# The first feed-forward of a hybrid encoder step begun with half of its token blocks

## Chip, cores and metric
One core of a Trainium2 chip runs the whole program in one launch. The metric is the device time of an execution in microseconds (us), from the median of three runs for the kernel before. TensorE, VectorE, ScalarE (ACT), GpSimd (POOL) and SyncE (SP, which issues the DMAs) run beside each other and wait for each other on semaphores.

## The reference, cut to what matters
A one-layer encoder step on 1088 tokens (1024 of a prompt, conditioned on one vector, and 64 of a sample, on another), 1024 features, in float32:

```
mod = silu(c) @ w_ada + b_ada            -> shift, scale, gate for 3 sub-layers
h   = rms_norm(x, gain) * (1 + scale) + shift
x  += 1/2 * gate * (silu(h @ Wg) * (h @ Wu)) @ Wd          (first half-step, width 2816)
x  += gate * (stick-breaking attention and retention, 8 + 4 heads) @ w_out
x  += 1/2 * gate * the same kind of feed-forward            (second half-step)
```

The change is in the opening of the two feed-forwards: norm, modulation, and the first tiles of `h @ [Wg Wu]`.

## The kernel before, in words
Activations lie feature-major: `A[k]` holds 128 features by 1088 tokens, for k of 0 to 7. The tokens are cut into four blocks of 272 (`BL`), numbered 0 to 3. Every float32 operand of a product is split into a high part (a cast by ACT, L81 and L228) and a low part (the difference, on POOL at L86 for weights and on VectorE at L229 for activations), and each product is three matmuls (`mm3`, L198 to L202).

The up-projection (class `Up`, L449) multiplies by Strassen-Winograd: k is halved (k and k+4), the tokens are paired (blocks 0 and 1 with blocks 2 and 3: half s=0 of a product is the columns of blocks 0 and 2, half s=1 those of blocks 1 and 3), and the outputs are paired as gate and up. A tile f (22 of them) has seven products in the order p1, p6, p5, p7, p2, p4, p3 (`ORDER`, L34), each for two halves s, each of 4 k by 3 matmuls of 272 columns. Its operands are seven combinations of activation blocks (b11, t1, t2, b21, t3, t4, b22; `x_parts`, L403), built once, and seven of weights per tile (`prep`, L477: four loads of 256 KB, four sums on VectorE at L469, seven splits). `read` (L511) takes a product out of PSUM with adds on VectorE (L521), copies and Silu on ACT (L533, L537, L546) and multiplies gate and up (L527).

Four raw and seven split weights fit, so one tile's weights are live at a time and the next tile's take the places as its products end.

In the opening of the first feed-forward (L628 to L726) SP loads x in three chunks of columns (`CHUNKS`, 24 loads), 16 loads of 512 KB of the modulation weights, of which four fit at a time (tag au), and the weights of tile 0. ACT squares x (L265), POOL and VectorE add the squares (L268), TensorE sums them over the partitions (`fold`), POOL takes the power (`factors`, L218), and TensorE spreads the row factors over the partitions (`rows`, L224), chunk after chunk. VectorE scales all of A by them (`scaled`, L673). TensorE makes the shift and scale vectors kt by kt (`ada_sums`, L681; `ada_turn`, L692; VectorE takes them at L685, L695, L697). `x_build_whole` (L432) builds the operands of one k for all four blocks at once, 544 columns wide: ACT applies scale and shift (L419), VectorE makes the differences (L424), and each of the seven is split. Behind each k, TensorE runs that k of p1, p6 and p5 of tile 0 for both halves. Then the remaining products of tile 0 and the tiles 1 to 21 follow with both halves of each product in turn; tiles 1 to 18 share VectorE with 64 long products for the later modulation vectors (`Ada`, L754).

The opening of the second feed-forward (L1308 to L1431) is cut by blocks already: operands of blocks 0 and 2 first (`build_first`), and at L1405 to L1431 tile 0 and tile 1 on half 0, tile 1 and tile 0 on half 1, with the weights of tile 0 split again for the last.

The order of the instructions on each engine is made by the scheduler of the program's framework, by the written order as priority and by what it takes to be ready. Inside `manual_schedule(engines={PE})` TensorE keeps the written order; the other engines don't. `high_priority(offset=2000)` moves the priority of what is in it 2000 steps ahead.

Of the kernel before, what the change touches and what calls it, by code (L numbers as in the profile page):

```python
# [8 lines left out]
F32 = mybir.dt.float32  # L9
# [106 lines left out]
def tile_hybrid_step(ctx: ExitStack, tc: tile.TileContext, I, O):  # L116
# [133 lines left out]
    class Norm:  # L250
# [92 lines left out]
    def ada_bias(s):  # L343
        bias = tiny.tile([P, KT], F32, tag="bias", name=f"bias{s}", bufs=2)
# [47 lines left out]
    def x_whole(pool):  # L392

        tags = [(hpool, f"{t}{k}") for k in range(KT) for t in "HL"] + [(pool, f"xe{i + 2}") for i in range(4)]
        for k in range(4):
            for i, name in enumerate(("b11", "b21", "t3", "t4", "b22", "t2", "t1")):
                if i < 5:
                    p, tag = tags[5 * k + i]
                else:
                    p, tag = xpool, f"A{k + 4 * (i - 5)}"  # L400
                yield k, name, p, tag

# [29 lines left out]
    def x_build_whole(k, n, pool, places):  # L432

        h = 2 * BL
        b = x_parts([(name, kt, lo, A[kt][:, lo:lo + h], None) for name, kt, lo in
                     (("b11", k, 0), ("b12", k, h), ("b21", k + 4, 0), ("b22", k + 4, h))], pool, n, k, "", True)
        for name in ("b11", "t2", "t1", "t3", "b21", "t4", "b22"):
            p, tag = places[k, name]
            t = p.tile([P, NTOK], F32R, tag=tag, name=f"x{name}{k}", bufs=1)
            split_h(b[name], t[:, :h], t[:, h:], nc.vector)  # L440
            for part in range(2):
                for s in range(2):
                    X[name, part, k, s] = t[:, (2 * part + s) * BL:(2 * part + s + 1) * BL]

    def x_split(b, names, k, s):
        for name in names:
            split_h(b[name], X[name, 0, k, s], X[name, 1, k, s], nc.vector)

# [110 lines left out]

    class Down:  # L560
# [68 lines left out]
    places = {(k, name): (p, tag) for k, name, p, tag in x_whole(xe)}  # L629
    up = Up(1, I["wup1"], hd[:FFT])  # L630
    with tc.tile_pool(name="st", bufs=1, reuse_waits="tile") as pool:
# [6 lines left out]

        def ada_load(kt):
            for s in (1, 0):  # L640
                t = adau[s, kt] = pool.tile([P, D], F32, tag="au", name=f"au{s}_{kt}", bufs=4)
# [16 lines left out]
        for kt in PAIRS[2:]:  # L658
            ada_load(kt)
        nc.sync.dma_start(qkg, I["qkg"])  # L660

        ns = [Norm(0, c, pool, ("pj", "z", "wt")[c]) for c in range(3)]

        def norm_first(c):
            ns[c].fold()
            ns[c].factors()
            ns[c].rows(("pj", "z", "wt")[c])

        def scaled(c, kts):

            c0, w = CHUNKS[c]
            for kt in kts:
                nc.vector.tensor_tensor(A[kt][:, c0:c0 + w], A[kt][:, c0:c0 + w], ns[c].rb[:, :w], op=ALU.mult)  # L673
# [881 lines left out]
```

## Time and profile before

| | us |
|---|---|
| median of 3 runs (lowest, highest) | 2296.6 (2291.3, 2299.8) |
| the profiled execution: its time | 2298.47 |
| its span, first to last instruction | 2296.7 |
| TensorE busy | 2184.1 (95%) |
| VectorE busy | 1503.6 (65%) |
| GpSimd busy | 1051.9 (46%) |
| ScalarE busy | 844.5 (37%) |

The busy time of TensorE is that of matmuls which overlap in the pipeline. The mean granted clock of the span is 0.979 of 2.4 GHz. A line such as "L202 PE MATMUL p<-xt,wh1s" names the line of the kernel, the engine, the operation, and the tiles it writes and reads by their names in the program.

### The profile page before, as it was taken

Reading aid. Unit: us, or ns where it says so; the run is one execution under the profiler, and the core shown is the slowest. Engines: PE = TensorE matmul, PEld = TensorE weight load, DVE = VectorE, ACT = ScalarE, POOL = GpSimd, SP = SyncE. Lnnn points to the kernel's source line nnn. Section 1 sums busy time; section 2 is a strip of 40 time slices with the busy share of each in tenths; the row PEclk is TensorE's granted clock in tenths of the full one; section 3 lists DMA queues with packets and bytes.
Section 4 is the critical chain, followed back from the end, with each engine's and each line's share of the span. In section 5 each row is a group of like instructions: output and inputs, shape, how many; then the busy total and the mean of one; then the engine's idle time right before and its main releaser. Section 6 shows DMA issues by size and latency. Waiting matters only on the chain.

```text
span 2296.7 us, 40613 instructions
## 1 busy us (share of the span) xinstructions
PE 2184.1 (95%) x15356; PEld 2140.8 (93%) x15356; DVE 1503.6 (65%) x2934; ACT 844.5 (37%) x1755; POOL 1051.9 (46%) x989
## 2 busy tenths in 40 slices
PE   5899999999999988888999999998999999999999
PEld 4899999999999988887888998997999999999999
DVE  6767677655787777787775446576555555556666
ACT  5533322332221336665664334365323232322211
POOL 3444444453454556444344445554544444534442
PEclk9899999999999989999999999999999999999999
DMA  7233333336344311110101112432222222352323
GB/s 249 93 126 126 116 127 113 131 108 218 119 129 132 120 52 61 35 41 21 44 22 62 37 41 77 153 99 92 95 85 94 84 90 81 108 178 84 101 82 103
DMA packets 119492, 225.63 MB, mean 98 GB/s; under 512 B 14848, under 2 KB 55808, under 8 KB 119296
## 3 DMA queue, kind: packets, MB, share of 16 engines
q1 hardware_dynamic: 119296, 223.03, 30.0%
q8 instruction: 121, 1.98, 0.4%
q14 instruction: 75, 0.61, 0.1%
HBM read 180.12 MB, written 42.86 MB: 97 GB/s over the span
## 4 chain that ended last, share of the span: by engine, by line
PE 80%; DVE 8%; POOL 4%; issue 4%; ACT 3%; DMA 1%; SPq 0%; POOLq 0%; DVEq 0%; ACTq 0%
PE p L201 13%; PE p L200 13%; PE p L202 13%; PE dn L200 8%; PE dn L201 7%; PE dn L202 7%; PE pj L200 3%; PE pj L202 3%; PE pj L201 3%; DVE f L961 2%; DVE s L964 1%; ACT f L953 1%; PE av L1006 1%; POOL rh L218 1%; PE wt L995 1%
## 5 line engine op out<-in xcount | busy, mean ns | idle before, releaser
L246 DVE SCALAR_TENSOR_TENSOR A<-dn,mod,A 128x384 f32<-128x384 f32 (+1 forms) x704 | 329.8, 497 | 147.7 <-PE dn L202 147.2
L200 PE MATMUL dn<-hs,wh 128*128 128x384 f32 (+1 forms) x1056 | 348.6, 330 | 5.2 <-DVE A L246 5.2
L201 PE MATMUL dn<-hs,wl 128*128 128x384 f32 (+1 forms) x1056 | 348.0, 330 | 0.0
L202 PE MATMUL dn<-hl,wh 128*128 128x384 f32 (+1 forms) x1056 | 347.8, 329 | 0.0
L86 POOL TENSOR_TENSOR wl<-wr,wh 128x512 fp32r<-128x512 f32 x178 | 242.9, 1373 | 143.2 <-ACT wh L81 140.0
L200 PE MATMUL pj<-Hh,wh 128*128 128x384 f32 (+1 forms) x672 | 237.8, 354 | 2.5 <-DVE A L246 2.5
L229 POOL TENSOR_TENSOR hl<-hr,hs 128x384 fp32r<-128x384 f32 x132 | 132.3, 1019 | 235.1 <-ACT hs L228 219.7
L202 PE MATMUL pj<-Lh,wh 128*128 128x384 f32 (+1 forms) x672 | 224.3, 334 | 0.0
L201 PE MATMUL pj<-Hh,wl 128*128 128x384 f32 (+1 forms) x672 | 223.3, 332 | 0.0
L200 PEld LDWEIGHTS dn<-hs,wh 128*128 128x128 f32 x1056 | 199.0, 188 | 5.6 <-DVE A L246 5.5
L201 PEld LDWEIGHTS dn<-hs,wl 128*128 128x128 f32 x1056 | 199.0, 188 | 0.0
L202 PEld LDWEIGHTS dn<-hl,wh 128*128 128x128 f32 x1056 | 199.0, 188 | 0.0
L228 ACT CAST hs<-hr 128x384 fp32r<-128x384 f32 x132 | 65.3, 496 | 326.6 <-PE dn L201 161.6
L521 DVE TENSOR_TENSOR u<-p,p 128x272 f32<-128x272 f32 x176 | 77.4, 440 | 161.2 <-PE p L202 161.2
L81 ACT CAST wh<-wr 128x512 fp32r<-128x512 f32 x178 | 107.7, 619 | 133.3 <-PE dn L202 39.5
L200 PE MATMUL p<-xt,wh1s 128*128 128x272 f32 x528 | 153.8, 291 | 0.9 <-DVE u L521 0.9
L202 PE MATMUL p<-xt,wh1s 128*128 128x272 f32 x528 | 153.6, 291 | 0.6 <-DVE xt L229 0.4
L201 PE MATMUL p<-xt,wl1s 128*128 128x272 f32 x528 | 153.8, 291 | 0.0
L86 POOL TENSOR_TENSOR wl1a<-wr1a,wh1a 128x512 fp32r<-128x512 f32 x66 | 94.1, 1427 | 120.8 <-ACT wh1a L81 120.8
L86 POOL TENSOR_TENSOR wl2a<-wr2a,wh2a 128x512 fp32r<-128x512 f32 x69 | 91.7, 1330 | 108.8 <-ACT wh2a L81 106.9
L200 PEld LDWEIGHTS pj<-Hh,wh 128*128 128x128 f32 x672 | 129.4, 193 | 5.5 <-issue 3.5
L201 PEld LDWEIGHTS pj<-Hh,wl 128*128 128x128 f32 x672 | 129.6, 193 | 0.3
(311 smaller groups left out, 6711.3 us busy)
## 6 DMA issues: line engine op xcount, KB each, us to landing
wa<-in_wada SPq DMA_DIRECT2D x56, 512.0 KB, 3.7
hd<-hh SPq DMA_DIRECT2D x44, 544.0 KB, 2.8
wr2a<-in_wup SPq DMA_DIRECT2D x92, 256.0 KB, 2.7
wr1a<-in_wup SPq DMA_DIRECT2D x88, 256.0 KB, 2.8
wr<-in_wdn SPq DMA_DIRECT2D x88, 256.0 KB, 2.9
hr<-hd SPq DMA_DIRECT2D x88, 192.0 KB, 2.6
wr<-in_win SPq DMA_DIRECT2D x56, 256.0 KB, 2.7
wr<-in_wout SPq DMA_DIRECT2D x34, 256.0 KB, 2.9
```

The costliest lines, as they stand in the source:

```text
L81: self.nc.scalar.copy(h, raw)
L86: self.nc.gpsimd.tensor_tensor(l, raw, h.bitcast(F32), op=ALU.subtract)
L200: nc.tensor.matmul(ps[:, :w], wh, xh, start=first, stop=False, skip_group_check=read_between)
L201: nc.tensor.matmul(ps[:, :w], wl, xh, start=False, stop=False, skip_group_check=read_between)
L202: nc.tensor.matmul(ps[:, :w], wh, xl, start=False, stop=last, skip_group_check=read_between)
L218: nc.gpsimd.tensor_tensor(out, a[:k, :n], neghalf[:k, :n], op=ALU.pow)
L228: nc.scalar.copy(hi, src)
L229: eng.tensor_tensor(lo, src, hi.bitcast(F32), op=ALU.subtract)
L246: nc.vector.scalar_tensor_tensor(A[d][:, s0:s0 + sw] if out is None else out[:, s0 - c0:s0 - c0 + sw], ps[:, s0 - c0:s0 - c0 + sw], mod[:, ...
L521: nc.vector.tensor_tensor(new(name), ps[:, :BL], v[y, s], op=ALU.add)
L953: nc.scalar.activation(t[:rows, end - k0:end - k0 + w], z[:rows, :w], AF.Sigmoid, scale=qsc[self.p][:rows, k, 2 * i + e:2 * i + e + 1])
L961: nc.vector.tensor_tensor_scan(fr[:, ::-1], fr[:, ::-1], fr[:, ::-1], 1.0, op0=ALU.mult, op1=ALU.bypass)
```

## The change
The first feed-forward is opened as the second is. x is loaded by blocks, 0 and 2 first; their norm, scaling, modulation and operands come first (`norm_first(0)`, `build(k, 0)`), and TensorE runs p1, p6 and p5 of tile 0 on half 0 behind each k. Then come norm and operands of blocks 1 and 3 (`norm_first(1)`, `build(k, 1)`), beside `up_first`: the rest of tile 0 and tile 1 on half 0, tile 1 and then tile 0 on half 1, with tile 0's weights prepared a second time. The operands of a pair of blocks are built 544 columns wide in fewer buffers (U twice, T once). The second feed-forward calls `up_first` too; there its first three products are now written ahead of their reads, and the reads of the two half-0 passes get a raised priority. The later modulation products go to tiles 2 to 19 instead of 1 to 18.

```diff
-            sq = self.pool.tile([P, 384 if self.n < 2 else w], F32, tag="acc" if new else "sq",
-                                name=f"sq{self.n}_{self.c}_{d}", bufs=4 if new else 3)
+            tag, bufs = ("v", 12) if self.n == 0 else ("acc", 4) if new else ("sq", 3)
+            sq = self.pool.tile([P, 384 if self.n == 1 else w], F32, tag=tag, name=f"sq{self.n}_{self.c}_{d}",
+                                bufs=bufs)
...
-        bias = tiny.tile([P, KT], F32, tag="bias", name=f"bias{s}", bufs=2)
+        bias = tiny.tile([P, KT], F32, tag="bias", name=f"bias{s}", bufs=1)
...
+    def x_pairs(k, s, n, x, rb, pool, places):
+        U = pool.tile([P, 6, BL], F32, tag="U", name=f"U{n}{k}{s}", bufs=2)
+        T = pool.tile([P, 2, BL], F32, tag="T", name=f"T{n}{k}{s}", bufs=1)
+        t2, b22, b21, t4 = (U[:, i] for i in (0, 3, 4, 5))
+        fu = U.rearrange("p j x -> p (j x)")
+        for i, (dst, at) in enumerate(((U[:, 1:3], (BL, 2 * BL)), (U[:, 3:5][:, ::-1, :], (4 * BL, 3 * BL)))):
+            kt = k + 4 * i
+            nc.vector.tensor_tensor(dst, x[i], rb, op=ALU.mult)
...
+                nc.scalar.activation(fu[:, c0:c0 + w], fu[:, c0:c0 + w], AF.Identity,
+                                     bias=mod[:, 3 * n, bt, kt:kt + 1], scale=scale_a[:, n, bt, kt:kt + 1])
+        nc.vector.tensor_tensor(T, U[:, 2:4], U[:, 1:3], op=ALU.subtract)
+        nc.vector.tensor_tensor(t2, b22, T[:, 0], op=ALU.subtract)
+        nc.vector.tensor_tensor(t4, b21, t2, op=ALU.subtract)
+        pl = places()
+        for src, names, i in ((U[:, 0:2], ("t2", "b11"), 0), (T, ("t1", "t3"), 2), (U[:, 4:6], ("b21", "t4"), 4)):
+            split_h(src, pl[i], pl[i + 1], nc.vector)
...
+        split_h(b22, pl[6][:, 0], pl[6][:, 1], nc.vector)
...
+    def up_first(up):
+        prep = up.prep(1)
+        for i, p in enumerate(ORDER):
+            if i > 2:
+                up.product(0, p, 0)
+            with tc.high_priority(offset=2000):
+                up.read(0, p, 0)
+            next(prep, None)
+        drain(prep)
+        for p in ORDER:
+            up.product(1, p, 0)
+            with tc.high_priority(offset=2000):
+                up.read(1, p, 0)
+        prep = up.prep(0)
+        for k in range(4):
+            for p in ORDER[:3]:
+                up.product(1, p, 1, [k])
+        for p in ORDER[:3]:
+            up.read(1, p, 1)
+            next(prep, None)
+        for p in ORDER[3:]:
+            up.product(1, p, 1)
+            up.read(1, p, 1)
+            next(prep, None)
+        drain(prep)
+        prep = up.prep(2)
+        for p in ORDER:
+            up.product(0, p, 1)
+            up.read(0, p, 1)
+            next(prep, None)
+        drain(prep)
...
-        for c, (c0, w) in enumerate(CHUNKS):
-            for k in range(KT):
-                nc.sync.dma_start(A[k][:, c0:c0 + w], I["x"][k][:, c0:c0 + w])
+        for b in (0, 2):
+            x_load(b, range(KT))
         for kt in PAIRS[:2]:
             ada_load(kt)
...
-        for kt in PAIRS[2:]:
-            ada_load(kt)
+        for i in range(2, KT, 2):
+            for kt in PAIRS[i:i + 2]:
+                for b in (1, 3):
+                    x_load(b, [kt - 1])
+                ada_load(kt)
+        for b in (1, 3):
+            x_load(b, [3, 7])
...
+        def norm_first(s):
+            for blk in (s, s + 2):
+                for d in range(KT):
+                    ns[blk].square(d)
+                ns[blk].fold()
+                ns[blk].factors()
+            rb[s] = pool.tile([P, 2, BL], F32, tag="rb", name=f"rb0_{s}", bufs=1)
+            for i, blk in enumerate((s, s + 2)):
+                ns[blk].rows("z" if s == 0 else "ms")
+                nc.scalar.copy(rb[s][:, i], ns[blk].rb[:, :BL])
...
         with tc.manual_schedule(engines={mybir.EngineType.PE}):
-            for c in range(3):
-                for d in range(KT):
-                    ns[c].square(d)
-                norm_first(c)
-                if c > 0:
-                    scaled(c - 1, PAIRS)
+            norm_first(0)
...
             for k in range(4):
-                scaled(2, PAIRS[2 * k:2 * k + 2])
+                build(k, 0)
...
                     for p in ORDER[:3]:
-                        for s in range(2):
-                            up.product(0, p, s, [k - 1])
-                x_build_whole(k, 0, pool, places)
+                        up.product(0, p, 0, [k - 1])
             for p in ORDER[:3]:
-                for s in range(2):
-                    up.product(0, p, s, [3])
+                up.product(0, p, 0, [3])
+        norm_first(1)
+        for k in range(4):
+            build(k, 1)
+        up_first(up)
...
-                for f in range(1, ADA1 + 1):
-                    up.tile(f, lambda f, i: ada.upto((7 * (f - 1) + i + 1) / (7 * ADA1)))
+            for f in range(2, ADA1 + 2):
+                up.tile(f, lambda f, i: ada.upto((7 * (f - 2) + i + 1) / (7 * ADA1)))
...
-    prep = up.prep(1)
-    for p in ORDER:
+    for p in ORDER[:3]:
         up.product(0, p, 0)
-        up.read(0, p, 0)
-        next(prep, None)
-    drain(prep)
...
+    up_first(up)
```

## Rows read from the trace of the kernel before

**Rows 1.** By stretch: length, busy PE, PEld, DVE, ACT, POOL (instructions), clock, DMA, GB/s
```profile
0.00:20.00 20.00, 4.91 (x21) 4.65 (x21) 5.26 (x11) 11.09 (x23) 9.97 (x21) 1.00 0.86 279
20.00:80.00 60.00, 43.97 (x396) 36.89 (x397) 52.18 (x108) 36.80 (x66) 16.36 (x13) 0.84 0.49 171
60.00:80.00 20.00, 13.52 (x52) 11.27 (x51) 19.44 (x30) 16.00 (x29) 5.05 (x3) 0.51 0.25 79
80.00:100.00 20.00, 19.11 (x150) 18.79 (x149) 12.48 (x23) 8.04 (x15) 10.78 (x8) 0.98 0.40 134
```

**Rows 2.** TensorE's timeline: start, duration, engine, line, tiles, count [wait before]
```profile
31.66 1.93 PE L681 MATMUL pa<-au,cS 128*32 128x128 f32 x32
...
52.17 0.37 PE L200 MATMUL p<-xb,wh1a 128*128 128x272 f32 x1
...
81.81 0.39 PE L200 MATMUL p<-xt,wh1s 128*128 128x272 f32 x1 [0.89 <-DVE u L521]
...
535.62 0.29 PE L202 MATMUL p<-xb,wh1s 128*128 128x272 f32 x1
```

**Rows 3.** Busy time by stretch, products of the up-projection alone, steady part
```profile
100.00:200.00 100.00, 100.00 (x799) 1.00 0.36 116
```

**Rows 4.** SP's timeline: the loads of x
```profile
2.18 12.38 SPq L646 DMA_DIRECT2D A<-in_x  x24
```

**Rows 5.** Groups by line and shape, VectorE, 0 to 130 us: busy, mean ns | idle before
```profile
L229 DVE TENSOR_TENSOR xt<-hn0t,xt 128x544 fp32r<-128x544 f32 x16 | 12.0, 782 | 0.0
L229 DVE TENSOR_TENSOR xb<-hn0b,xb 128x544 fp32r<-128x544 f32 x12 | 8.6, 715 | 0.0
L673 DVE TENSOR_TENSOR A<-A,rb 128x384 f32<-128x384 f32 x16 | 8.1, 544 | 2.5 <-PE rb L224 2.5
L424 DVE TENSOR_TENSOR hn0t<-hn0b,hn0t 128x544 f32<-128x544 f32 x8 | 6.6, 823 | 0.3 <-ACT hn0b L419 0.2
L424 DVE TENSOR_TENSOR hn0t<-hn0b,hn0b 128x544 f32<-128x544 f32 x8 | 6.1, 768 | 0.0
L469 DVE TENSOR_TENSOR wr1a<-wr1a,wr1a 128x512 f32<-128x512 f32 x8 | 5.5, 688 | 1.2 <-POOL wl1a L86 1.2
...
L697 DVE TENSOR_SCALAR scale_a<-mod,gains 128x2 f32<-128x2 f32 x8 | 3.5, 444 | 0.0
L673 DVE TENSOR_TENSOR A<-A,rb 128x320 f32<-128x320 f32 x8 | 3.5, 480 | 0.3 <-PE rb L224 0.3
L685 DVE COPY pe<-pa 128x256 f32<-128x256 f32 x8 | 3.4, 420 | 2.4 <-PE pa L681 2.2
...
L695 DVE TENSOR_SCALAR mod<-pm,bada 128x2 f32<-128x2 f32 x16 | 2.7, 212 | 0.9 <-PE pm L692 0.9
```

**Rows 6.** TensorE's timeline, second feed-forward: first product, last row factors, last product
```profile
1543.02 0.37 PE L200 MATMUL p<-xe,wh2a 128*128 128x272 f32 x1
...
1547.81 1.03 PE L224 MATMUL rb<-ident,rx 128*128 128x128 f32 x6
...
2028.88 0.29 PE L202 MATMUL p<-x1A,wh2s 128*128 128x272 f32 x1
```

**Rows 7.** Busy time by stretch, products alone, opening of the second feed-forward
```profile
1543.00:1580.00 37.00, 26.74 (x162) 0.86 0.11 33
```

**Rows 8.** TensorE's waits, 1543 to 1607 us: us in total, times, longest
```profile
PE p L200 <- DVE u L521: 5.7, 6, 2.2
PE p L200 <- ACT g L537: 2.8, 1, 2.8
```

**Rows 9.** POOL's timeline, first feed-forward: two low parts of weights
```profile
58.07 3.04 POOL L86 TENSOR_TENSOR wl1a<-wr1a,wh1a 128x512 fp32r<-128x512 f32 x2 [12.44 <-ACT wh1a L81]
```

**Rows 10.** VectorE's timeline: the same small write without and with POOL's work beside it
```profile
38.77 0.22 DVE L697 TENSOR_SCALAR scale_a<-mod,gains 128x2 f32<-128x2 f32 x1
...
60.14 0.99 DVE L697 TENSOR_SCALAR scale_a<-mod,gains 128x2 f32<-128x2 f32 x1
```

**Rows 11.** POOL's timeline, second feed-forward: a low part of tile 1's weights
```profile
1560.79 2.00 POOL L86 TENSOR_TENSOR wl2s<-wr2s,wh2s 128x512 fp32r<-128x512 f32 x1 [10.75 <-ACT wh2s L81]
```

More of the change, by code (lines that the diff above doesn't have):

```diff
@@ L390, in over_x @@
         put(A[kt], keys)
[L392 to L401, printed above, removed]
     def x_parts(parts, pool, n, k, s, whole, kept=()):
@@ L430, in x_parts @@
         return b
[L432 to L441, printed above, removed]
-                for s in range(2):
-                    X[name, part, k, s] = t[:, (2 * part + s) * BL:(2 * part + s + 1) * BL]
     def x_split(b, names, k, s):
@@ L628, in tile_hybrid_step @@
     xe = tc.alloc_tile_pool(name="xe1", bufs=1, reuse_waits="tile")
-    places = {(k, name): (p, tag) for k, name, p, tag in x_whole(xe)}
     up = Up(1, I["wup1"], hd[:FFT])
+    up.pool = tc.alloc_tile_pool(name="u1", bufs=2, reuse_waits="tile")
     with tc.tile_pool(name="st", bufs=1, reuse_waits="tile") as pool:
@@ L657, in tile_hybrid_step @@
                                 axis=mybir.AxisListType.X, op=ALU.add)
-        for kt in PAIRS[2:]:
-            ada_load(kt)
-        nc.sync.dma_start(qkg, I["qkg"])
[L662 to L673, printed above, removed]
+        for i in range(2, KT, 2):
[5 more added lines that the diff above has]
+            x_load(b, [3, 7])
+        nc.sync.dma_start(qkg, I["qkg"])
+        ns = [Norm(0, b, up.pool, ("pj", "wt", "z", "av")[b], (b * BL, BL)) for b in range(4)]
+        rb = {}
+        def norm_first(s):
[8 more added lines that the diff above has]
+                nc.scalar.copy(rb[s][:, i], ns[blk].rb[:, :BL])
         def ada_sums(kt):
@@ L698, in ada_turn, with halves, places, build @@
                                         op0=ALU.add, op1=ALU.mult)
-        with tc.manual_schedule(engines={mybir.EngineType.PE}):
-            for c in range(3):
-                for d in range(KT):
-                    ns[c].square(d)
-                norm_first(c)
-                if c > 0:
-                    scaled(c - 1, PAIRS)
+        def halves(p, tag):
+            t = blocks(p.tile([P, NTOK], F32R, tag=tag, name=f"x{tag}", bufs=1))
+            return [t[:, 0:2], t[:, 2:4]]
+        HL = [f"{t}{k}" for k in range(KT) for t in "HL"]
+        free = [[h for tag in HL[:14] for h in halves(hpool, tag)],
+                [h for tag in HL[14:] for h in halves(hpool, tag)] + [h for i in range(4) for h in halves(xe, f"xe{i}")]]
+        def places(k, s):
+            over = [h for kt in (k + 4, k) for h in halves(xpool, f"A{kt}")] if s == 1 else []
+            return over + [free[s].pop(0) for _ in range(7 - len(over))]
+        def build(k, s):
+            x_pairs(k, s, 0, [blocks(A[kt])[:, s::2, :] for kt in (k, k + 4)], rb[s], pool, lambda: places(k, s))
+        with tc.manual_schedule(engines={mybir.EngineType.PE}):
+            norm_first(0)
             for kt in PAIRS[:2]:
@@ L760, in tile_hybrid_step @@
     ADA1, ADA2 = 18, 18
[L761 to L775 removed]
+    with tc.tile_pool(name="ada", bufs=1, reuse_waits="tile") as apool:
+        ada = Ada(apool, (2, 4, 3, 5))
+        with tc.manual_schedule(engines={mybir.EngineType.DVE}):
+            for f in range(2, ADA1 + 2):
+                up.tile(f, lambda f, i: ada.upto((7 * (f - 2) + i + 1) / (7 * ADA1)))
+    dpool = tc.alloc_tile_pool(name="d1", bufs=2, side="right", reuse_waits="tile")
+    down = Down(dpool, U_DN1, hd[:FFT], 2)
+    for f in range(ADA1 + 2, FFT):
+        up.tile(f, down.ahead if f == FFT - 1 else None)
+    up.pool.release()
     xe.release()
```

52 lines of the change are left out of this document (16 added, 36 removed).

## The prediction

> **What bounds the kernel now.** I began with the busy time by stretch of the opening [rows 1]. In the first 20 us TensorE is busy for 4.91 us. From 20 to 80 us VectorE is busy for 52.18 of 60 us and TensorE's 43.97 us are mostly small or slow work: from 60 to 80 us it issues 52 matmuls at a mean granted clock of 0.51, which is the lower of its two levels (1.2 GHz) for nearly all of the time. From 80 to 100 us it is busy for 19.11 us at 0.98 (2.4 GHz). So the opening is bound by what makes the operands (loads, norm, modulation vectors, then VectorE), and the rest of the first up-projection by TensorE.
>
> TensorE's timeline gives the marks [rows 2]: the modulation sums start at 31.66 us, the first product at 52.17, and the last wait before the steady part ends at 81.81 us; the last product is issued at 535.62. The products' own rate in the steady part is 799 in 100 us, 0.1252 us each [rows 3]. A tile of the up-projection has 7 products x 2 halves x 4 k x 3 matmuls = 168, and 22 tiles have 3696, or 462.7 us. By 81.81 us three of the seven products of tile 0 were done for both halves, 72 matmuls. 81.81 - 72 x 0.1252 = **72.8 us** is the dead time of TensorE: 72.8 + 462.7 = 535.5, and the last product confirms it. Nothing after 81.81 us in this stage waits. So the change is worth what it takes from these 72.8 us, plus what it does to the opening of the second feed-forward, whose code it shares.
>
> **What the change does, step by step.**
>
> *Loads.* The 24 loads of x take SP 12.38 us to issue, 0.516 each [rows 4]. Of the new 32, only the 16 of blocks 0 and 2 come first: 8.3 us, with half the bytes. The other 16 stand in SP's queue between the modulation weights, which wait for their buffers, and the last four behind the last of those. Nothing needs them before the second norm, so they cost nothing as long as the first build covers them; without that cover the second norm starts late by one wait of the modulation chain, a few us.
>
> *Norm.* Three rounds over 1088 columns end when the modulation sums start, 31.66 us. Two rounds over half of the columns lie between half of that, 15.8 us, and two thirds, 21.1. A round is a chain of short steps that hardly shrink with the columns, so I take 20 us, near the upper end.
>
> *First half of the operands.* The VectorE work of the build before, by line [rows 5]: low parts (L229) 12.0 + 8.6, differences (L424) 6.6 + 6.1, scaling (L673) 8.1 + 3.5, together 44.9 us. The change keeps the elements and groups them anew (pairs of blocks, the row factors copied to SBUF by four more ACT copies, which lie beside VectorE); so 22.4 us a half. With the first half go all of the modulation work, 3.4 + 2.7 + 3.5 = 9.6 us, four weight sums at 0.69 = 2.8, and six additions of squares of blocks 1 and 3, at half of a 544-wide difference (0.77) some 0.4 each, 2.4. That is 37.2 us. Such durations overlap a little at their ends: those of 20 to 80 us add up to about 57 against 52.18 of busy time, so I multiply by 0.91: 34 us. With 3 us for links of the chain that nothing fills, the first half is done at 20 + 34 + 3 = **57 us**. By then 27 matmuls of tile 0 have run (three products, k of 0 to 2).
>
> *Second half.* 22.4 us of build, four sums for tile 1 at 0.69 = 2.8, and the reads of two tiles' first halves, 2 x 7 operations at 0.4 = 5.6: 30.8, times 0.91 = 28, and a little waiting: **86 us**. Meanwhile TensorE has 168 - 27 + 27 = 168 matmuls to do before it needs the last k, 21 us; if it finds them ready it has 195 done at 86 us, and the dead time is 86 - 24.4 = 61.6, **11.2 us less** than now. That is one end.
>
> *The other end* is in this trace already: the second feed-forward opens in this very order (tile 0 and tile 1 on the first half, tile 1 and tile 0 on the second, tile 0's weights split twice). There the first product is at 1543.02 and the last at 2028.88 [rows 6], 486.0 us with its own end, against 462.7: 23.3 us lost. Only 162 products fit into its first 37 us, at a mean clock of 0.86 [rows 7]. Carried over, a start at 57 - 27 x 0.1252 = 53.6 and 23.3 lost give a dead time of 76.9, 4.1 us **more** than now. Two things are better in the new place. The second row factors reached the second feed-forward at 1548.8 [rows 6], 5.8 us after its start, and here they are there when the first half ends: 5.8 off. And the change raises the priority of the first half's reads, so that they don't queue on VectorE and ACT behind the build: of the waits for them, 5.7 and 2.8 us [rows 8], I take off 3. So 76.9 - 8.8 = 68.1, **4.7 us less** than now. I take this value, since the same order of work has been measured there, and keep both ends.
>
> *Weights.* Tile 0's weights are loaded and split a second time (7 casts on ACT, 7 low parts on POOL, 4 sums, 4 loads). In the stretch after 81.81 us these engines have room; it is in the 23.3 already. If that cover goes, the 7 low parts cost up to 7 x 1.52 = 10.6 us [rows 9].
>
> *Second feed-forward.* Three products of tile 0 are put ahead and the reads raised. Between nothing and the whole 8.5 us of waits [rows 8] lies what this gives; only the reads of two first halves are moved, so I take **3.5 us**. Below nothing: raised reads push the build back by some 14 short operations, but they must run anyway. I allow 2 us.
>
> *Nothing:* one buffer fewer for the bias, the squares in the v buffers, the modulation parts one tile later: all lie under a steady TensorE. If they showed, VectorE would be late in the steady part, and it has over a third of its time free from 80 to 100 us [rows 1].
>
> Sum: 4.7 + 3.5 = 8.2 us. The profiled execution took 2298.5 us, 1.9 above the median of 2296.6, which I forecast from: **2288**.
>
> *A rule against the change.* While POOL made two low parts from 58.07 to 61.11 us [rows 9], a VectorE write of 128x2 numbers took 0.99 us instead of 0.22 [rows 10]. The change puts seven low parts of tile 1 beside the second half's build, when VectorE is the bound. The forecast counts them only as far as the factor 0.91 holds such delays. The Trainium skill (SBUF — State Buffer, section SBUF: two separate sides) calls the port pair of the two engines an exclusive lock, held for a whole instruction by whichever starts first when VectorE reads two SBUF operands. The delayed write agrees in kind.
>
> **Rivals.**
> 1. *Only the builds bind.* TensorE finds tile 1 ready: 11.2 us from the first opening and the 5 us of the two long waits from the second, 16.2: 2280. For it: in the steady part a tile's weights are never late. Against it: in the second feed-forward the low part of tile 1's second weight came after POOL had idled 10.75 us for its cast [rows 11].
> 2. *POOL and VectorE exclude each other.* All of the 10.6 us of low parts are added to the second half: it ends at 96 instead of 86, the first opening loses 4.7 - 10.6 = -5.9, the second gives 3.5: 2.4 slower, 2299. The delay of 0.77 us behind a low part of 1.52 speaks for half of it. This is the lock of the Trainium skill (SBUF — State Buffer, SBUF: two separate sides) taken at its full length.
> 3. *Tile 1's weights wait behind the build* (slower). Only reads are raised; sums and casts of tile 1 are written after the four builds. If they run after them, TensorE ends tile 0's first half at about 64 us, gets 12 matmuls of tile 1, and has 96 done at 90 us (86, a sum, a cast, a low part). Dead time 90 - 12.0 = 78, and what the second feed-forward lost after its first 37 us, 23.3 - (37 - 162 x 0.1252) = 6.6, makes 84.6: 11.8 slower, 8.3 with the second's gain, **2305**. It decides if the first sum of tile 1 starts after about 80 us. For it: that late cast [rows 11]. Against it: there the sums ran inside the build.
> 4. *The order is not what the text suggests.* Only TensorE keeps the written order; if work of the second half is placed ahead of the first, products begin no earlier and nothing changes: 2297.
>
> **How the numbers follow.** Forecast 0.42 (its own range 2282 to 2293), rival 1 0.26, rival 2 0.15, rival 3 0.12, rival 4 0.05. A measurement of this kernel can tell about 0.5%, 11.5 us, from no change, so faster means under 2285.1: nearly all of rival 1 and a good fifth of the forecast, 0.35. Slower means over 2308.1: the bad part of rival 3 and some of what I don't see, 0.07. The rest, 0.58, is within. The range goes from below rival 1 to just under rival 3: 2276 to 2303.
>
> **What would show it.** Right: modulation sums near 20 us, the last k of the first half near 57 us, VectorE busy over 85% until about 86 us, and TensorE with some 165 to 195 products done by then; the last product of the first up-projection near 531 us. In the second feed-forward, shorter waits for reads. Wrong: a first half after 62 us (norm or loads misjudged); TensorE idle from 64 us on for a weight of tile 1 (rival 3); low parts and VectorE alternating without overlap (rival 2); a steady part that is no longer steady, from the second split of tile 0 or the modulation parts.

## The result and the profile after

The changed kernel takes **2311.2 us** (median of 6 runs, 2307.9 to 2316.6) against 2297.4 (6 runs, 2291.3 to 2302.8) for the kernel before: ratio 1.0064, 95% interval 1.0049 to 1.0079. It is slower by 0.6%, little but clear of the scatter; the forecast, 2288 within 2276 to 2303, was wrong. The profiled execution took 2311.4, near its median, so its trace can stand for the runs.

| us | before | after | difference |
|---|---|---|---|
| start to last product of the first up-projection | 535.6 | 556.8 | +21.1 |
| from there to the first product of the second one | 1007.4 | 998.3 | -9.1 |
| second up-projection, first to last product | 485.9 | 487.1 | +1.2 |
| the rest | 267.8 | 267.2 | -0.6 |
| span | 2296.7 | 2309.4 | +12.7 |

The loss is in the first opening. Busy time by stretch of the changed kernel's opening (columns as in [rows 1]):

```profile
20.00:40.00 20.00, 10.73 (x142) 8.41 (x141) 16.33 (x27) 7.04 (x13) 6.72 (x5) 1.00 0.67 227
40.00:60.00 20.00, 14.86 (x165) 12.81 (x166) 14.65 (x42) 11.18 (x19) 1.81 (x2) 0.93 0.69 228
60.00:80.00 20.00, 17.40 (x89) 16.67 (x89) 12.51 (x24) 10.15 (x25) 12.41 (x11) 0.55 0.15 53
80.00:102.00 22.00, 10.78 (x52) 8.55 (x52) 21.57 (x39) 18.95 (x40) 2.23 (x2) 0.68 0.00 1
102.00:120.00 18.00, 18.00 (x134) 18.00 (x134) 9.56 (x18) 6.88 (x13) 9.16 (x8) 0.91 0.43 147
```

VectorE, which was to be busy throughout, has 5.35 us free from 40 to 60 and 7.49 from 60 to 80, and is full only from 80 to 102. TensorE is idle for half of that last stretch, 11.2 of 22 us. Its granted clock of 0.55 from 60 to 80 us is no news: it was 0.51 there before [rows 1]. The marks on its timeline, which answer to [rows 2]:

```profile
20.16 1.94 PE L736 MATMUL pa<-au,cS 128*32 128x128 f32 x32
...
36.86 1.94 PE L736 MATMUL pa<-au,cS 128*32 128x128 f32 x32 [6.52 <-DVE pe L740]
...
45.33 1.93 PE L736 MATMUL pa<-au,cS 128*32 128x128 f32 x32 [2.12 <-DVE pe L740]
...
95.10 0.59 PE L200 MATMUL p<-xA,wh1a 128*128 128x272 f32 x1 [5.55 <-ACT xA L228]
...
98.11 0.59 PE L200 MATMUL p<-xH,wh1s 128*128 128x272 f32 x1 [1.34 <-ACT wh1s L81]
...
556.77 0.29 PE L202 MATMUL p<-xxe,wh1s 128*128 128x272 f32 x1
```

The modulation sums start at 20.16 us, as forecast. Then TensorE's sums wait for VectorE to copy the sums before them (`pe`), 11.2 us in all from 18 to 60 us (2.3 us in the kernel before), mostly because the copy stands in VectorE's queue behind a build. VectorE's and POOL's timelines beside each other in the build of k = 0 and at the two ends of the second half's work:

```profile
31.82 1.50 DVE L449 TENSOR_TENSOR U<-U,T 128x272 f32<-128x272 f32 x1
33.36 1.39 DVE L450 TENSOR_TENSOR U<-U 128x272 f32<-128x272 f32 x1
34.68 1.79 DVE L229 TENSOR_TENSOR xH<-U,xH 128x544 fp32r<-128x544 f32 x1
36.39 0.41 DVE L740 COPY pe<-pa 128x256 f32<-128x256 f32 x1
...
67.28 0.42 DVE L229 TENSOR_TENSOR xL<-U,xL 128x272 fp32r<-128x272 f32 x1
...
77.45 0.72 DVE L439 TENSOR_TENSOR U<-A,rb 128x544 f32<-128x544 f32 x1 [2.15 <-ACT rb L728]
...
100.93 0.71 DVE L229 TENSOR_TENSOR xxe<-U,xxe 128x544 fp32r<-128x544 f32 x1
```

```profile
31.65 1.38 POOL L86 TENSOR_TENSOR wl1s<-wr1s,wh1s 128x512 fp32r<-128x512 f32 x1 [9.12 <-ACT wh1s L81]
32.99 2.89 POOL L86 TENSOR_TENSOR wl1s<-wr1a,wh1s 128x512 fp32r<-128x512 f32 x2
...
61.10 2.78 POOL L86 TENSOR_TENSOR wl1a<-wr1a,wh1a 128x512 fp32r<-128x512 f32 x2 [3.80 <-ACT wh1a L81]
...
98.13 1.30 POOL L86 TENSOR_TENSOR wl1s<-wr1s,wh1s 128x512 fp32r<-128x512 f32 x1 [22.43 <-ACT wh1s L81]
```

While POOL makes three low parts, from 31.65 to 35.9 us, a 272-wide VectorE operation takes 1.39 to 1.50 us (0.43 elsewhere) and a 544-wide one 1.79 (0.72 elsewhere). The first half is built at 67.7 us, the second starts at 77.45, when its row factors come, and ends at 101.6. The low part of tile 1's second weight comes at 98.13, after 22.43 us without work for POOL.

### The profile page after: what moved, and what is told of

The parts are those of the page before. It is cut to its first block, busy times and chain, and to the rows that moved or that the text cites. A ratio compares the mean times of both kernels' runs of the same rounds, so it can differ in the third digit from the quotient of the medians.

```text
span 2309.4 us, 40733 instructions
## 1 busy us (share of the span) xinstructions
PE 2182.8 (95%) x15374; PEld 2139.2 (93%) x15374; DVE 1513.7 (66%) x2949; ACT 852.1 (37%) x1782; POOL 1063.4 (46%) x1003
## 4 chain that ended last, share of the span: by engine, by line
PE 77%; DVE 9%; POOL 5%; issue 4%; ACT 3%; DMA 2%; SPq 0%; POOLq 0%; DVEq 0%; ACTq 0%
PE p L201 12%; PE p L200 12%; PE p L202 12%; PE dn L200 7%; PE dn L201 7%; PE dn L202 7%; PE pj L200 3%; PE pj L202 3%; PE pj L201 3%; DVE f L1023 2%; DVE s L1026 1%; ACT f L1015 1%; POOL rh L218 1%; PE av L1068 1%; PE wt L1057 1%
## 5 line engine op out<-in xcount | busy, mean ns | idle before, releaser
L202 PEld LDWEIGHTS pj<-Lh,wh 128*128 128x128 f32 x672 | 128.0, 190 | 0.4
L86 POOL TENSOR_TENSOR wl1s<-wr1s,wh1s 128x512 fp32r<-128x512 f32 x46 | 61.8, 1344 | 144.4 <-ACT wh1s L81 144.4
L86 POOL TENSOR_TENSOR wl2s<-wr2s,wh2s 128x512 fp32r<-128x512 f32 x46 | 61.0, 1326 | 133.5 <-ACT wh2s L81 130.7
```

The source lines that it names most:

```text
L86: self.nc.gpsimd.tensor_tensor(l, raw, h.bitcast(F32), op=ALU.subtract)
L202: nc.tensor.matmul(ps[:, :w], wh, xl, start=False, stop=last, skip_group_check=read_between)
```

## The experiments

Each kernel below has one profile and one timed run. "Last product" is that of the first up-projection, from the profile: 535.62 us in the kernel before, 556.77 in the changed one. Whole times stand beside a run of the kernel before on the same chip, and single ones differ by several us. Last products differ from trace to trace too: up to 200 us e4 runs the same instructions in the same order on TensorE, VectorE, ScalarE and GpSimd as the kernel before, and e11 the same as the changed kernel, and still their last products are 2.0 and 1.7 us apart. So a price of about 2 us, read from two single traces, is not clear of that.

**First round: which part of the change, and which wait.** e1 to e3 each mend one wait of the changed kernel; e4 is the kernel before with the second feed-forward's part alone.

```diff
 # e1: x of blocks 1 and 3 ahead of the later modulation weights
...
+        for b in (1, 3):
+            x_load(b, range(KT))
 # e2: copies of the sums on ACT
-                nc.vector.tensor_copy(pe, pa[:, :256])
+                nc.scalar.copy(pe, pa[:, :256])
 # e3: in up_first, first pass
             with tc.high_priority(offset=2000):
                 up.read(0, p, 0)
-            next(prep, None)
+                next(prep, None)
```

> Theory A (the second norm came 10 us too late, because the last four loads of x stand behind the modulation weights in SP's queue and ACT squares them last): with all 16 loads of blocks 1 and 3 ahead of those weights, the row factors of blocks 1 and 3 are there before the first half is built, the second build starts at about 67 us instead of 77.5 and ends near 92; the last product of the first up-projection moves from 556.8 to 547-549 us. Theory B (only tile 1's weights, split late, hold TensorE): the build moves but the last product stays within 2 us of 556.8.

> Theory A (the modulation chain waits on VectorE's queue: the copy of one sum out of PSUM ran 6.5 us late behind the build of k = 0, and each later k waits for its scale): with these copies on ACT, which idles there, the last scale is written at 51-53 us instead of 59.3 and the first half is built by 59-61 instead of 67.3 us; the rest moves by as much, last product 549-551 us. Rival (VectorE's own work bounds the first half): the first half still ends at 65-67 us and the last product at 555-557.

> Theory B (tile 1's sums and casts wait behind the second build, rival 3 of the prediction): with their priority raised like that of the reads, tile 1's low parts are made before 90 us, TensorE finds up to 72 matmuls (9 us) in its idle stretch from 84 to 98 us, and the last product moves from 556.8 to 548-551 us, although the second build ends a little later (102-104). Theory A alone (operands only): the last product stays at 555-558, for the end of the build decides.

> The kernel before with only the second feed-forward's part of the change. By the prediction's step (raised reads save 3.5 us there) the products of the second feed-forward take 482 us from first to last, instead of 485.9. By the trace of the changed kernel, where they took 487.1, they take 486-488, and the time is that of before within 3 us: the loss lies in the first opening alone.

| | last product | whole | before, same chip |
|---|---|---|---|
| e1 x early | 563.66 | 2315.9 | 2297.2 |
| e2 copies on ACT | 558.61 | 2311.6 | 2297.2 |
| e3 tile 1's weights raised | 554.50 | 2308.0 | 2297.2 |
| e4 second feed-forward alone | 537.59 | 2301.4 | 2297.2 |

e4 leaves the first opening as it was, so the loss belongs to the new first opening. (Its second up-projection took 488.4 us, just over the 486 to 488 expected, and its whole time is 4.2 us longer, not within 3.) No single repair recovers more than 2.3 us. e1 and e2 missed the numbers of both their theories, e3's 554.50 lies below theory A's range and short of theory B's. In e1 the waits of the sums for their copies grew from 11.2 to 14.8 us, 2.9 us of waits for the modulation weights, which now load later, came on top, and the first half was built at 80.8 us. In e2 the waits for copies became 8.8 us for ACT and 5.1 for VectorE's `scale_a`, and the first half was built at 66.8, as its rival had it. A repaired wait came back as the next one.

**Second round: the price of each suspect.** e5 puts all norms ahead; e6 and e7 take the modulation chain and POOL's low parts out; e8 tests the 9 us that came back later.

```diff
 # e5: e1, and in the written order of TensorE
             for kt in PAIRS[:2]:
                 ada_turn(kt)
+            norm_first(1)
...
+            norm_rows(1)
             for p in ORDER[:3]:
                 up.product(0, p, 0, [3])
-        norm_first(1)
...
 # e6: e5, for the last three pairs of k
-                        ada_sums(kt)
...
-                        ada_turn(kt)
+                        nc.vector.tensor_copy(mod[:, 0:2, :, kt], mod[:, 0:2, :, kt - k - 1])
+                        nc.vector.tensor_copy(scale_a[:, 0, :, kt], scale_a[:, 0, :, kt - k - 1])
 # e7: no low parts for tiles 0 and 1
-            self.w[f, name] = (h, wu.low(r, h, f"{self.n}{name}_{f}"))
+            self.w[f, name] = (h, h if self.n == 1 and f < 2 else wu.low(r, h, f"{self.n}{name}_{f}"))
 # e8: the kernel before, ahead of the modulation sums
+        for i in range(60):
+            nc.scalar.copy(cS, cS)
```

> The changed kernel with all of x loaded right behind tile 0's weights, and with the squares, sums and factors of blocks 1 and 3 put into TensorE's written order right after the first pair of modulation sums (in the changed kernel they stand behind all first-half products); only the spreading of their row factors stays late, before the last k of the first half. Theory A (the second norm comes too late: in the changed kernel the second build starts at 77.45 us, 10 us after the first half is built at 67.3): the second build starts by about 69 us, ends by about 93, and the last product of the first up-projection is issued at 547 to 550 us instead of 556.77. Rival B (VectorE is held by the modulation chain, and eight more squares and two more rounds of norm ahead of it delay the first half by as much): first half built after 75 us, last product at 556 to 565.

> The kernel of e5 without the modulation sums of the last three pairs of k: it leaves out their twelve loads, sums and turns and copies the modulation of k = 0 and 4 in their place (that part of the computation is changed). Theory C (the chain of sum, VectorE copy, turn, VectorE scaling, once for each k and queued in order behind the builds, holds the first half): first half built by about 50 us instead of 67.3, second by about 80, last product at 528 to 535. If the chain were only in the shadow of the builds (rival), it would give no more than the VectorE time of what is left out, some 6 us: last product within 6 us of e5's.

> The changed kernel, with the low parts of the weights of tiles 0 and 1 of the first up-projection left out (the high part is used twice, so that part of the computation is changed); the number of products is the same. POOL has then nothing to do beside the builds. Theory of exclusion (VectorE operations stretched from 0.72 to 1.79 us beside a low part): the build of k = 0 gets 3 us shorter, the first half is built by about 63 us, tile 1's weights are ready 2 us sooner, last product at 549 to 552. Rival (the low parts lie where VectorE or TensorE wait for something else): last product at 554 to 557.

> The kernel before, with sixty copies of the small silu operand onto itself put ahead of the modulation sums on ACT, so that its whole opening ends some 15 to 25 us later and all that follows is unchanged. The changed kernel and e1 to e3 took 995.7 to 998.3 us from the last product of the first up-projection to the first of the second, the kernel before and e4 1007.4 and about 1006, though TensorE's order of work there is the same. Theory P (the later start alone, by the moments at which the granted clock falls, makes the stretch shorter): 994 to 999 us here too. Rival Q (the new placing of the buffers, or the down-projection's first wait, makes it shorter): 1005 to 1008 us here.

| | last product | whole | before, same chip |
|---|---|---|---|
| e5 norms ahead | 559.54 | 2321.8 | 2293.2 |
| e6 e5 without the chain | 550.61 | 2314.6 | 2293.2 |
| e7 without low parts | 547.25 | 2302.7 | 2293.2 |
| e8 before, opening later | 551.32 | 2312.2 | 2293.2 |

e5 is rival B: the first half is built at 78.4 us, and the second build starts at 77.1, as late as in the changed kernel, and ends at 102.2. TensorE now waits for the squares of the two blocks put ahead, and the modulation comes later. Its waits from 18 to 60 us, and the row factors and the start of the second build:

```profile
PE st L276 <- POOL sq L269: 11.0, 2, 5.7
PE st L276 <- DVE sq L269: 3.5, 1, 3.5
PE pa L735 <- DVE pe L739: 3.3, 3, 2.0
```

```profile
75.47 0.39 ACT L727 COPY rb<-rb 128x272 f32<-128x272 f32 x1 [0.64 <-PE rb L224]
...
77.08 0.72 DVE L439 TENSOR_TENSOR U<-A,rb 128x544 f32<-128x544 f32 x1
```

So the late second norm, though it stands in the trace as a gap of 10 us, is no cause that can be had by itself: its work ahead of the first half delays that by as much. e6 gives 8.9 us against e5, more than its rival's 6 of VectorE's own work, but only a part of theory C's 25 to 30; with the norms ahead as in e5, that is what the chain costs, and no run takes it alone out of the changed kernel. e7 gives 9.5, more than the theory of exclusion had it (4.8 to 7.8). VectorE's groups by line and shape, 20 to 102 us, of the changed kernel:

```profile
L450 DVE TENSOR_TENSOR U<-U 128x272 f32<-128x272 f32 x8 | 6.0, 751 | 0.1
...
L449 DVE TENSOR_TENSOR U<-U,T 128x272 f32<-128x272 f32 x8 | 5.6, 705 | 0.0
```

and of e7:

```profile
L450 DVE TENSOR_TENSOR U<-U 128x272 f32<-128x272 f32 x8 | 3.5, 435 | 0.1
L449 DVE TENSOR_TENSOR U<-U,T 128x272 f32<-128x272 f32 x8 | 3.5, 433 | 0.0
```

The same sixteen operations, some of which run beside POOL's low parts in the changed kernel, take 11.6 us there and 7.0 without. VectorE's whole busy time from 20 us to the end of the second build falls from 65.1 to 59.2. That stretching fits the 5.2 us by which e7 is ahead when its second build ends (at 97.3 instead of 101.6 us, with 7 products more done). The other 4.2 come after it, up to 160 us; they may be tile 1's weights, whose low parts e7 takes away too, and no run separates them. So 9.5 us is the price of the low parts, not of the exclusion alone.

e8's stretch between the two up-projections is 1005.8 us, within rival Q's numbers: a later start, by 15.7 us here, does not give the 9 us back. They are taken up further on.

**Third round: is each price the change's?** The same two parts are left out of the kernel before (e9 as e6, e10 as e7); e11 is the first part of the change alone; e12 is e5 with the repairs of e2 and e3.

> The kernel before with the same part left out as in e6: the loads, sums and turns of the last three pairs of k, with the modulation of k = 0 and 4 copied in their place (that part of the computation is changed). It asks whether the price of the modulation chain, 8.9 us in e6 against e5, belongs to the change. Theory (it does: the builds over all blocks before are long enough to cover the chain): last product of the first up-projection at 531 to 536 us against 535.62. Rival (the chain holds both kernels alike): 524 to 529.

> The kernel before with the same part left out as in e7: the low parts of the weights of tiles 0 and 1 of the first up-projection (the high part is used twice, so that part of the computation is changed). It asks whether the price of the low parts, 9.5 us in e7 against the changed kernel, belongs to the change. Theory (most of it does, since in the changed kernel two tiles' low parts, not one's, stand beside the builds and late in the opening): last product at 531 to 535 us against 535.62. Rival (VectorE and POOL disturb each other as much before): 524 to 528.

> The changed kernel with the opening of the second feed-forward put back as it was before, the counterpart of e4. Theory (the two halves of the change add up; the raised reads give nothing): last product of the first up-projection within 2 us of 556.77, the second up-projection 485.5 to 486.5 us from first to last product instead of 487.1. Rival (the raised reads gain something behind the new first opening that they don't gain in e4): 488 or more.

> e5 (x early, all norms ahead) with the two other repairs: the copies of the modulation sums on ACT (e2) and tile 1's sums and casts raised with the reads (e3). Theory (each repair is worth little alone because the next wait takes its place; together they free VectorE's early gaps and tile 1's weights): last product at 547 to 553 us, still more than 10 us after the kernel before. Rival D (VectorE's and ACT's order is the limit however the pieces stand): 555 to 562. If the placement were only unlucky in the changed kernel, it would come below 540.

| | last product | whole | before, same chip |
|---|---|---|---|
| e9 before, without the chain | 533.29 | 2293.9 | 2292.0 |
| e10 before, without low parts | 532.96 | 2289.0 | 2292.0 |
| e11 first opening alone | 555.06 | 2307.0 | 2292.0 |
| e12 all moved | 554.81 | 2304.1 | 2292.0 |

e9, e10 and e11 came as their theories had it. Chain and low parts cost the kernel before 2.3 and 2.7 us, hardly more than two traces differ by; they cost the new order 8.9 and 9.5. e12 missed the theory's upper end by 1.8 us and is worth as little as e3 alone. (From 20 to 60 us the mean granted clock was 0.57 in e12 and e17, 0.61 in e15 and 0.66 in e2, between the two levels, against 0.97 in the changed kernel. In e15 the last modulation vector came at 58.1 us all the same, against 59.1 in the changed kernel.) In e11 the second up-projection takes 485.6 us, in e4 488.4. Over all traces, the six with the old opening of the second feed-forward have 485.2 to 486.7, the thirteen with the new one 485.9 to 490.6, in the mean 1.7 more: the new one gains nothing and costs a little. The waits that answer to [rows 8] in the changed kernel, 1555 to 1620 us:

```profile
PE p L200 <- ACT Hm L228: 6.7, 1, 6.7
PE p L200 <- ACT p L543: 2.6, 1, 2.6
```

TensorE hardly waits for VectorE's reads now, but 6.7 us for an operand of the second build; the seven raised reads of tile 0 ran on VectorE from 1562 to 1571 us, ahead of it.

**Fourth round: do the prices add up, and what is left.** e13 is e6 without low parts and with e3's repair; e14, its control, is the kernel before without chain and low parts.

> The kernel of e6 (x early, all norms ahead, the modulation of three pairs left out and copied), also without the low parts of tiles 0 and 1 as in e7 (both parts of the computation are changed), and with tile 1's sums and casts raised as in e3. It asks what is left of the 21.1 us when the chain, POOL and tile 1's weights are all taken from the opening. Theory (the prices add up): 559.5 - 8.9 - 9.5 - 2.3 = 539, last product at 536 to 542 us. Rival (they are partly the same time, counted twice, and what is left is VectorE's own work in two half-wide builds and their links): 543 to 549.

> The kernel before with the same two parts left out as in e13 (the modulation of three pairs and the low parts of tiles 0 and 1), as its control. Theory (2.3 us of e9 and 2.7 us of e10 add up, since builds over all blocks cover the rest): last product at 529 to 532 us against 535.62. Rival (each hid the other): below 527.

| | last product | whole | before, same chip |
|---|---|---|---|
| e13 new order, three out | 533.44 | 2295.0 | 2291.5 |
| e14 before, two out | 528.72 | 2289.5 | 2291.5 |

e13 came lower than either theory, e14 0.3 us under the first one's range. From e5 to e13 the last product comes 26.1 us earlier, from the kernel before to e14 6.9: with chain, low parts and late weights gone, 4.7 us of the 21.1 remain, and what they are stays open. So these three, with the norms ahead, carry 16.4 us of the loss. Together they cost more than singly (20.7), which fits that a wait taken away singly is partly replaced by one of the other two.

**Fifth round: TensorE's own order.** In the changed kernel the written order of TensorE is kept only up to the last k of the first half. After it the scheduler put products of tile 1 on the second build's operands (`xA` at 84.77 to 95.10 us) ahead of 72 matmuls on the first half's. e15 keeps the written order there too, e16 adds e3's repair, e17 e5's norms as well.

```diff
-        up_first(up)
+        with tc.manual_schedule(engines={mybir.EngineType.PE}):
+            up_first(up)
```

> The changed kernel with TensorE kept to the written order in the four passes of the first opening too (in the changed kernel its order there is the scheduler's, which puts twelve matmul groups of three on the second build's operands, tile 1's first product of the second half, ahead of 72 matmuls of tile 1's first half). Theory O (TensorE's 8.5 us of waits for those operands between 84 and 95 us come from that order): the waits go, and the last product comes at 550 to 553 us instead of 556.77. Rival W (tile 1's sums and casts, which come at 92 to 101 us, are as late as the operands): TensorE waits for a weight in their place, and the last product stays at 555 to 559.

> e15 with tile 1's sums and casts raised as in e3, so that TensorE has both the order and the weights of tile 1's first half. Theory O + W: TensorE finds 168 matmuls done when the second build ends; if that is at 102 us, the last product comes at 102 - 21.0 + 462.7 = 543.7, so 543 to 548. Rival V (VectorE: the raised sums and POOL's low parts beside the build make it end at 111 us, as in e3): 111 - 21.0 + 462.7 = 552.7, so 551 to 555, like e3's 554.50.

> e16 with x early and all norms ahead as in e5 (not the copies on ACT of e12). With e12 at 554.81 it asks whether the whole of what was found, without leaving anything out, brings the new order near the kernel before. Theory: the second build starts earlier and VectorE's gaps fill, 540 to 548 us. Rival V: VectorE and POOL in each other's way, 549 to 556; then no arrangement of these parts that was tried comes within 10 us of 535.62.

| | last product | whole | before, same chip |
|---|---|---|---|
| e15 written order | 558.46 | 2309.8 | 2290.8 |
| e16 and weights | 553.38 | 2302.7 | 2290.8 |
| e17 and norms | 555.34 | 2304.3 | 2290.8 |

All three went the rivals' way. In e15 the waits for `xA` are gone and one for a weight of tile 1 stands in their place (TensorE's timeline):

```profile
96.55 0.59 PE L200 MATMUL p<-xH,wh1s 128*128 128x272 f32 x1 [13.54 <-ACT wh1s L81]
```

In e16 TensorE has both, and does 140 products from 80 to 102 us instead of 52; but now the second build ends late:

```profile
110.10 0.71 DVE L229 TENSOR_TENSOR xxe<-U,xxe 128x544 fp32r<-128x544 f32 x1
```

Tile 1's sums and low parts then come between the two builds and beside the second one: it starts at 82.7 us instead of 77.5 and ends at 110.8 instead of 101.6. Either the weights of tile 1 wait for the build or the build waits for them. No arrangement tried without leaving work out came within 17 us of the kernel before in the first opening, and none beat it in whole time.

## Why the prediction was wrong

**Right.** Sums at 20 us (20.16). VectorE's work from 20 us to the end of the second build: 62 us forecast (34 + 28), 65.1 measured, of which 5.9 are the stretching that e7 takes away. The second build took 24.2 us where 29 were forecast (57 to 86), because tile 1's seven reads and three of its four weight sums fell outside it. The place, too: the loss lies in the opening, and after 160 us TensorE runs as steadily as before (800 products in 100 us). One reading was off without harm: by 81.81 us TensorE had started 77 products, not 72, which makes the dead time 72.2 us there and 73.0 at the last product.

**The step that failed: the idle time of VectorE.** The forecast gave "3 us for links of the chain that nothing fills", and "a little waiting" for the second half. From 20 to 101.7 us VectorE was idle for 16.6 us: 10.7 in the first half, 5.5 between the halves, 0.5 in the second (columns as in [rows 1]):

```profile
20.00:67.70 47.70, 31.16 (x333) 26.40 (x332) 37.03 (x77) 23.69 (x45) 15.13 (x12) 0.89 0.63 212
67.70:77.45 9.75, 9.28 (x42) 8.95 (x43) 4.24 (x10) 2.89 (x9) 5.80 (x7) 0.50 0.02 7
77.45:101.70 24.25, 13.03 (x70) 10.80 (x69) 23.78 (x43) 20.44 (x43) 1.94 (x2) 0.71 0.00 1
```

VectorE's waits in the kernel before, from the first modulation sum to the end of the builds (31.66 to 79.50 us):

```profile
DVE pe L685 <- PE pa L681: 2.2, 3, 1.0
DVE mod L695 <- PE pm L692: 0.9, 2, 0.5
...
DVE hn0t L424 <- ACT hn0b L419: 0.2, 1, 0.2
```

and in the changed kernel, from 20 to 67.7 us (the second line lies mostly ahead of 20 us):

```profile
DVE mod L750 <- PE pm L747: 4.5, 5, 1.1
DVE U L439 <- ACT rb L728: 3.6, 1, 3.6
DVE T L448 <- ACT U L446: 1.8, 2, 0.9
DVE pe L740 <- PE pa L736: 1.7, 2, 1.4
DVE ra L217 <- PE st L276: 1.6, 1, 1.6
```

In the kernel before a build of one k covers all blocks, and the next sums, copies and turns pass under it: VectorE waits 3.3 us for them and for ACT's scaling behind them, and leaving three of the four pairs out gives 2.3 us (e9). A half-wide build is half as long, and the chain of sums, copy, turn and scale is as long as it was: VectorE waits 8.0 us for the same steps while it builds half as much, and the price became 8.9 (e5 to e6). The forecast halved the work and kept the cover. The 5.5 us between the halves belong to a second term that failed: the second row factors were to be "there when the first half ends", and they came 9.8 us after it.

**The step that was mis-sized: POOL.** Rival 2 priced the exclusion at 10.6 us and had a chance of 0.15; the forecast counted it "only as far as the factor 0.91 holds such delays". All low parts of the two tiles together cost 9.5 us (e7), of which about 5 fit the stretched operations, and 2.7 in the kernel before (e10). [Rows 9, 10] showed it for one small write; here it met the large operations of the builds. But it was not the place that rival 2 named: tile 0's low parts met the first half's builds, and tile 1's came almost all before or after the second (one beside it, at 98.13 us). That its 10.6 comes near 9.5 is luck. The Trainium skill (SBUF — State Buffer, section SBUF: two separate sides) has the pair of ports that VectorE and GpSimd share taken for a whole instruction by whichever starts first, where VectorE reads two SBUF operands. The trace fits that on both sides: 1.79 us instead of 0.72 is 1.07 more, less than one low part of 1.38, and the copy from PSUM at 36.39 us, with POOL busy until 37.1, kept its 0.41.

**Rival 3, tile 1's weights.** Its test was whether the first sum of tile 1 starts after 80 us. Two sums ran at 73.9, so by that test it was not met; but the next came at 92.3, and POOL idled for 22.43 us. Its size, 12 us slower, was nearest to what happened. The test named the first weight, and the second decides. Raising the weights gives 2.3 us (e3), hardly more than two traces differ by, since what they gain the build loses (e16). Of rival 4 one sentence was true where the forecast did not look: past the first half TensorE does not keep the written order either; but keeping it gives nothing while the weights are late (e15).

**Counted through the dead time.** The forecast's good end was 61.6 us. The second build ended 15.7 us later than 86; of 195 products then possible 117 were done, 78 x 0.1252 = 9.8; and 7.0 us more were lost after it, 6.5 of them up to 160 us, of which 4.1 in waits for VectorE's reads and a low part and some at a granted clock of 0.91. 61.6 + 15.7 + 9.8 + 7.0 = 94.1, and 556.8 - 462.7 is 94.1. The other end, 76.9 from the second feed-forward, was no bound: that opening has its modulation vectors ready, and the first one has to make them. This was the choice that set the range too low.

**Second feed-forward.** A gain of 3.5 us was forecast and 1.2 were lost; the sentence that raised reads "must run anyway" overlooked that an operand of the build, behind them, is what TensorE then waits for.

**What came back.** The 9.1 us between the up-projections were in no term. 5.0 of them are there when the projections begin, 3.1 in the down-projection's first wait (5.2 us before, 2.1 after; 2.6 to 3.0 in the variants of the kernel before, so part of that is the one trace). 4.6 lie in the next 84 matmuls of the projections, which take 28.1 us before and 23.5 after, with the same instructions in the same order; later gains and losses nearly cancel. Busy time of the 10 us behind TensorE's next wait there, and the first product behind that wait, before:

```profile
824.44:834.44 10.00, 10.00 (x39) 9.63 (x40) 7.41 (x15) 2.38 (x6) 4.19 (x5) 0.53 0.13 43
```

```profile
824.44 0.41 PE L200 MATMUL pj<-Hh,wh 128*128 128x384 f32 x1 [2.47 <-DVE A L246]
```

and after:

```profile
840.58:850.58 10.00, 9.62 (x60) 9.08 (x60) 9.28 (x20) 3.69 (x9) 5.23 (x6) 1.00 0.17 62
```

```profile
840.58 0.41 PE L200 MATMUL pj<-Hh,wh 128*128 128x384 f32 x1 [1.92 <-DVE A L246]
```

In the 10 us behind the wait TensorE does 60 matmuls instead of 39, at a granted clock of 1.00 instead of 0.53 (the levels are 1.2 and 2.4 GHz).

## What to carry to other kernels

When a long step is cut in halves so that work can start on the first, the work of the engines halves, but a chain of short steps that ran under the long one keeps its length: price that chain against the shorter cover, not against the old one. Two engines that hold each other up are priced by what stands beside what after the move; an operation that is stretched shows by its mean duration in the groups by shape. Where mending the longest wait gives nothing, take two or three suspects out at once, with the same cut in the old kernel as control; here it took both to see 16 of the 21 us.

## What the runs showed of the hardware

Ahead of the projections TensorE waits 4.4 us for row factors in every kernel here, old order or new, and from the first product behind it the next 115 instructions of TensorE are the same in all. In the 20 us after it the mean granted clock was 0.67 in nine of the nineteen traces (the kernel before, every variant of it, and e5, e6 and e13) and 0.88 to 0.96 in the other ten; the first 84 matmuls of the projections take 28.0 to 28.1 us in the nine and 22.2 to 23.5 in the ten. Neither the order of work there, nor the new placing of buffers (e5), nor the start time (e8 at 828.8 us has 0.67, e16 at 827.8 has 0.96) sorts them. What does differ is a second fall of the clock: it falls in or behind the 4.4 us wait and rises again in all nineteen, and in the nine it falls once more behind the next wait, which lasts 2.08 to 2.47 us there and 2.05 or less in the ten. Whether the longer wait brings the second fall, or both follow from the moment of the first, no run separates. It is worth 4.6 to 5.8 us of a whole run, a third to nearly half of what this change cost, and it stands in the whole times above (e5, e6 and e13 are among the nine, the changed kernel is not), so a small difference between kernels should be looked for stage by stage.
